# Dividing the last PSUM copy between ScalarE and VectorE, with fewer counting instructions, in a batched matrix product

## The chip, the cores and the metric

One core of one Trainium2 chip. The metric is the device time of a whole execution in microseconds (us), taken as the median of several runs. "Span" is the profiler's time from the first to the last instruction of one execution, 1.8 us less than the device time here.

## The reference

```python
batch, m, k, n = 16, 512, 768, 1024          # x: (16, 768, 512), y: (16, 768, 1024), fp32
def reference(x, y):
    return np.einsum('bkm,bkn->bmn', x, y).astype(np.float32)
```

## The kernel before

Per batch, SyncE loads x (1.5 MB) and y (3 MB), VectorE casts both to bf16, TensorE runs 48 matmuls of 512 columns in two groups, ScalarE copies each group out of PSUM (the memory of the tile ps, which the matmuls write), and SyncE stores the 2 MB result. In the trace all transfers go through one hardware queue (q1 on the page: 4512 packets, 109.05 MB), they land in the order in which SyncE issues them, and each ends in 16 landings (768 for the 48 transfers), which I take as one from each of the 16 DMA engines.

```python
NO = 5                                                        # five output buffers ob
ps = [psum [P, HB=2, NT=2, NF=512] fp32 for i in range(2)]    # a group: 2 blocks of 1024 fp32 a partition
...
    for _ in range(60):                                       # the counting instructions
        nc.vector.sem_inc(idle, 1)
    for b in range(B):                                        # casts
        ...
        nc.vector.tensor_copy(yb[:, i, ks], ys[i][:, ks]).then_inc(cast, 1)
...
    nc.scalar.nop().then_inc(room, 2)
    for _ in range(60):
        nc.scalar.sem_inc(idle, 1)
    for b in range(B):
        if b >= NO:
            nc.scalar.wait_ge(so[b % NO], 16 * (b // NO))     # the buffer's last store has landed
        for g in range(2):
            nc.scalar.wait_ge(groups, 2 * b + g + 1)          # the matmuls of this group are done
            cp = nc.scalar.copy(ob[b % NO][:, g * HB:(g + 1) * HB]..., ps[g][:])
            if b < B - 1:
                cp.then_inc(room, 1)
        ...
    section.close()                                           # all engines meet here
    nc.sync.dma_start(o_v[B - 1], ob[(B - 1) % NO][:])        # the last store
```

Nothing ever waits for `idle`: the counting instructions only shift what comes after them (in the trace they take 0.067 us each on ScalarE and 0.093 on VectorE). In the queue, blocks of four stores stand between the loads, and at the end the stores of batches 8 to 14 stand one behind the other, with the store of batch 15 after the closing barrier.

## Time and profile before

| | before |
|---|---|
| device time, median of 3 runs | 260.51 us (260.50 to 260.77) |
| span of the profiled run | 258.8 us |
| bytes moved | 109.05 MB, DMA engines busy 98.6% of the span |
| matmuls end / last copy ends / last store issued | 249.58 / 251.48 / 251.67 us |
| last data packet ends / span ends | 257.57 / 258.8 us |

The prediction below shows the lines that carry this. A line of the timeline reads: start, duration, engine, line of the program, operation, output from input, and in brackets the idle time ahead of it with what ended it. I also use two kinds of record beneath those views: the DMA packets (start, duration, size) and the landings (the 16 semaphore increments per transfer). For the last store the 16 landings come 0.38 to 0.46 us after the ends of the 16 rows of packets in the kernel before and 0.33 to 0.47 in the changed one, both in order of time, so I read the spread of the landings as how far the DMA engines have drifted apart. The records do not number the engines.

### The profile page before, as it was taken

To read this page: it belongs to the slowest core of one execution; us is meant where nothing else is said; L and a number is where in the kernel's file an instruction comes from. 1 tells how busy PE (TensorE), PEld (TensorE's weight loads), DVE (VectorE), ACT (ScalarE), POOL (GpSimd) and SP (SyncE) were. 2 spreads that over 40 slices of the span, in tenths; PEclk is the share of its full clock that TensorE was granted. 3 is DMA by queue.
4 is the path that set the end of the run, shared out by engine and by line. 5 is a ranking of instruction groups with operands and counts; after the bars stand their busy time and mean duration, and the time that the engine had idled before them with its cause. 6 is when DMAs were issued, how large, how long until landed. Compare 5 with 4: busy or idle time off the path is not lost. (4 is left out here: it accounts for less than half of the span.)

```text
span 258.8 us, 2506 instructions
## 1 busy us (share of the span) xinstructions
PE 181.6 (70%) x768; PEld 89.3 (34%) x768; DVE 82.0 (32%) x33; ACT 60.9 (24%) x33; POOL 0.2 (0%) x4
## 2 busy tenths in 40 slices
PE   0009999999999006999499920899669980099950
PEld 0004555554545002454145500355325530035520
DVE  0261645527164350011734525002255262300000
ACT  1000442234220005222214002324402200413430
POOL 0000000000000000000000000000000000000000
PEclk9999999999999855899779985699979995569995
DMA  7999989899999999999999989999899999999987
GB/s 273 424 475 410 471 380 479 372 479 395 456 410 441 387 418 430 466 446 418 433 433 425 471 352 443 420 461 479 372 479 403 448 410 390 433 438 420 436 357 324
DMA packets 4514, 109.07 MB, mean 421 GB/s; under 512 B 768, under 2 KB 768, under 8 KB 768
## 3 DMA queue, kind: packets, MB, share of 16 engines
q1 hardware_dynamic: 4512, 109.05, 98.6%
q14 instruction: 2, 0.02, 0.0%
HBM read 75.50 MB, written 33.55 MB: 421 GB/s over the span
## 5 line engine op out<-in xcount | busy, mean ns | idle before, releaser
L157 PE MATMUL ps<-yb,xb 128*128 x768 | 181.6, 402 | 68.0 <-PEq L152 68.0
L157 PEld LDWEIGHTS ps<-yb,xb 128*128 x768 | 89.3, 116 | 159.8 <-issue 89.8
L173 ACT COPY ob<-ps 128x2048 f32<-128x2048 f32 x32 | 59.6, 1872 | 185.3 <-PE ps L157 125.2
L135 DVE CAST yb<-ys 128x6144 bf16<-128x6144 f32 (+1 forms) x17 | 53.8, 3172 | 77.8 <-DMA ys<-in_y_dram 77.8
L131 DVE CAST xb<-xs 128x3072 bf16<-128x3072 f32 x16 | 28.2, 1761 | 62.5 <-DMA xs<-in_x_dram 48.7
L173 ACT ACT_TABLE_LOAD x1 | 1.3, 1283 | 5.3 <-issue 5.3
L203 POOL MEMSET const-bfloat16-1.0<- 128x1 bf16 x1 | 0.1, 103 | 0.0
L203 POOL MEMSET const-uint8-127<- 128x1 uint8 x1 | 0.1, 102 | 0.0
L203 POOL MEMSET const-float32-0.0<- 128x1 f32 x1 | 0.1, 100 | 0.2 <-issue 0.2
L203 POOL MEMSET const-float32-1.0<- 128x1 f32 x1 | 0.1, 99 | 0.0
## 6 DMA issues: line engine op xcount, KB each, us to landing
ys<-in_y_dram SPq DMA_DIRECT2D x16, 3072.0 KB, 18.6
out_dram<-ob SPq DMA_DIRECT2D x16, 2048.0 KB, 27.2
xs<-in_x_dram SPq DMA_DIRECT2D x16, 1536.0 KB, 20.1
```

The lines of the kernel that those rows point to most:

```text
L131: nc.vector.tensor_copy(xb[:, i], xs[i][:]).then_inc(cast, 1)
L135: nc.vector.tensor_copy(yb[:, i, ks], ys[i][:, ks]).then_inc(cast, 1)
L157: mm = nc.tensor.matmul(ps[g][:, m, nt], x_w[:, bass.ds(s, 1), kt, mo], yb[:, bass.ds(s, 1), kt, nt * NF:(nt + 1) * NF], start=(kt == 0), ...
L173: cp = nc.scalar.copy(ob[b % NO][:, g * HB:(g + 1) * HB].rearrange("p m (t f) -> p m t f", f=NF), ps[g][:])
L203: nc = _bacc.Bacc("TRN2", target_bir_lowering=False, num_devices=1)
```

## The change

The intent is to shorten the last step ahead of the last store: VectorE, idle by then, takes one block of the last group while ScalarE copies the other. The counting instructions fall from 60 to 16 on each of the two engines.

```diff
-    for _ in range(60):
+    for _ in range(16):
         nc.vector.sem_inc(idle, 1)
...
+    nc.vector.wait_ge(so[(B - 1) % NO], 16 * ((B - 1) // NO))
+    nc.vector.wait_ge(groups, 2 * B)
+    nc.vector.tensor_copy(ob[(B - 1) % NO][:, MT - 1].rearrange("p (t f) -> p t f", f=NF), ps[1][:, HB - 1])
...
-    for _ in range(60):
+    for _ in range(16):
         nc.scalar.sem_inc(idle, 1)
...
-            cp = nc.scalar.copy(ob[b % NO][:, g * HB:(g + 1) * HB].rearrange("p m (t f) -> p m t f", f=NF),
-                                ps[g][:])
+            h = HB if (b, g) < (B - 1, 1) else HB - 1
+            cp = nc.scalar.copy(ob[b % NO][:, g * HB:g * HB + h].rearrange("p m (t f) -> p m t f", f=NF),
+                                ps[g][:, :h])
```

## The prediction

> **What bounds the kernel now.** I read the page first (span, busy slices, queues), then the chain of waits, then the timeline of the last 60 us, and last the trace's single records of semaphores and DMA packets.

> The page of the kernel before:

> ```profile
> span 258.8 us, 2506 instructions
> PE 181.6 (70%) x768; PEld 89.3 (34%) x768; DVE 82.0 (32%) x33; ACT 60.9 (24%) x33; POOL 0.2 (0%) x4
> PEclk9999999999999855899779985699979995569995
> DMA  7999989899999999999999989999899999999987
> q1 hardware_dynamic: 4512, 109.05, 98.6%
> q14 instruction: 2, 0.02, 0.0%
> ```

> The 16 DMA engines are busy for 98.6% of the span and move 109.05 MB: for almost the whole time this kernel is bound by its transfers, and VectorE (32%) and ScalarE (24%) have room. Only the edges of the DMA row, the leading 7 and the closing 8 and 7, leave something to win. The queue of instructions made two transfers; they return below. The PEclk row shows half clock after TensorE's pauses, at the 5 5 6 near the end too.

> The chain that ended last, in order of time:

> ```profile
> 225.71 0.27 issue
> 225.98 23.61 PE ps L157 x96
> 249.59 0.02 issue
> 249.61 1.87 ACT ob L173
> ```

> So the end hangs on the matmuls of the last two batches and then on one ScalarE copy of 1.87 us, the copy that the change cuts. The timeline shows what stands ahead of and behind it:

> ```profile
> 202.04 1.87 ACT L173 COPY ob<-ps 128x2048 f32<-128x2048 f32 x1 [3.25 <-PE ps L157]
> 202.04 1.76 DVE L131 CAST xb<-xs 128x3072 bf16<-128x3072 f32 x1 [1.80 <-PE ps L157]
> 207.87 3.36 DVE L135 CAST yb<-ys 128x6144 bf16<-128x6144 f32 x1 [4.07 <-DMA ys<-in_y_dram]
> ...
> 223.74 3.63 ACT L173 COPY ob<-ps 128x2048 f32<-128x2048 f32 x2 [19.83 <-DMA out_dram<-ob]
> ```

> ```profile
> 244.49 1.87 ACT L173 COPY ob<-ps 128x2048 f32<-128x2048 f32 x1 [3.37 <-PE ps L157]
> 249.61 1.87 ACT L173 COPY ob<-ps 128x2048 f32<-128x2048 f32 x1 [3.26 <-PE ps L157]
> 251.67 0.33 SPq L188 DMA_DIRECT2D out_dram<-ob  x1
> ```

> The copy ends at 251.48, the final 2 MB store is issued at 251.67 (0.19 us of barrier), its first data packet starts at 252.50 (0.83 us after the issue), its last ends at 257.57, and the span ends at 258.8. Two things in the packet records decide how much an earlier issue is worth. Fourteen of the 16 engines finish the store of batch 14 between 251.45 and 251.84, so they idle for 0.7 to 1.1 us. The other two finish it at 252.41 and 252.45 and hardly idle at all. In the final store each engine moves 8 packets of 16 KB, 0.61 us each, 4.9 us in all.

> The row at 223.74 shows the same coupling once more: ScalarE had waited 19.83 us for the store of batch 8 to land, so that a buffer came free, and TensorE's start at 225.98 hangs on that copy.

> [...] The trace before has no VectorE read of PSUM, [...] a cast of 3072 takes 1.76 us and one of 6144 takes 3.36, that is 0.52 ns an element and 0.16 us fixed. [...]

> [...]

> [...] the two refills in the span, at 8.97 and 10.91 us, are packets of 8 KB[...].

> [...] the first group of batch 14 takes 8.06 us from 225.98, full clock comes back at 231.48, and each later group takes 5.34.

> **The change part by part.** (1) The last ScalarE copy shrinks from 2048 to 1024 elements a partition. Half of 1.87 is 0.93; with a fixed part of up to 0.2 us kept, about 1.02 us. It is on the path. (2) VectorE gets a copy of 1024 fp32 out of PSUM[...]. It waits for the same semaphore as ScalarE, and the rows at 202.04 show that both engines start within the same 0.01 us on such a release. VectorE has been idle since 222.3. So the pair ends at 249.61 + 1.23 = 250.84 instead of 251.48: 0.64 us saved, with VectorE now the later of the two. (3) The closing barrier: before, SyncE had collected VectorE's and TensorE's drains at 249.66 and waited for ScalarE alone. Now VectorE's arrives last and SyncE asks for it first, so one semaphore step that used to be hidden, about 0.06 us between neighbouring SyncE records, comes after it. Issue at 250.84 + 0.19 + 0.06 = 251.09, so 0.58 us earlier. (4) From there to the end. First data could come at 251.09 + 0.83 = 251.92. The fourteen engines are then nearly all free, but the two late ones start their eight packets at about 252.45 as their queues allow, and end at 252.45 + 4.92 = 257.37 instead of 257.57. Worth 0.20 us if they stay late, the full 0.58 if they do not.

> (5) The 44 counting instructions fewer on each engine. They cost 0.067 us each on ScalarE and 0.093 on VectorE, 3.0 and 4.1 us together, but off the path: VectorE's ended at 6.46, the first x load's last engine reported at 7.15, and the first cast began at 7.18. ScalarE's first copy is at 26.4. No saving there. What they do move is the refill of instructions. ScalarE's even steps of 0.067 us have one gap, of 0.377, ahead of its 64th instruction, the last count; VectorE's 64th is its first cast. The two refills follow about 4 us later. With 44 fewer, the 64th instruction becomes, by counting, VectorE's cast of the last x (at 212.4) and ScalarE's second last copy (at 244.5). Both have slack: the y behind that cast lands at 218.8, and that ScalarE copy ends over 3 us before the next group is done. So a hiccup of 0.3 us in each is hidden. But a refill also holds up the one DMA engine that carries it: the data packets behind the two refills began 0.3 us late and took 1.16 and 1.46 us against the usual 0.91, so 0.55 and 0.86 us each, and on queues that never empty such a delay stays. At least one of the two late engines may be late for this reason. Moving the refills may free them, or make others late nearer the end.

> Sum: between 0.20 and 0.58 us for the copy, and 0 to 0.3 on top if an earlier landing of batch 8 lets TensorE start earlier. I take 0.38 us of 260.51, which is 260.13.

> **The rivals.** (a) The late DMA engines eat the gain: the store is issued 0.58 us earlier, yet the end moves 0.2. For it: the two end times above[...]. Time 260.3. (b) The refills' move frees those engines: full gain and an earlier start of TensorE. For it: the delays at 8.97 and 10.91. Against it: the stores stay in the queue ahead, so the end cannot come before 251.84 + 4.92 = 256.76, 0.8 us at most. Time 259.7. (c) A refill stalls the last copy or the barrier: for it, the second last ScalarE copy is only one instruction from the boundary by my count. 0.3 to 1 us lost: 260.5 to 261. (d) VectorE's read of PSUM is slower than estimated; beyond 1.87 us it would undo the change. Against it: ScalarE's 0.91 ns an element from the same memory. [...]

> **Range and chances.** The middle is 260.13. The smallest plausible gain, with the spread of the runs (260.5 to 260.77), gives 260.6; the largest, (b), gives 259.7. Two per cent is 5.2 us, six times what the gap at the end can yield; slower by 5 us would need a stall that nothing in the profile suggests. So within 2% at 0.98.

> **What would show it.** Right: a ScalarE copy of about 1.02 us and a VectorE copy of about 1.23 in the timeline, both from about 249.6; the last store's issue about 0.6 us earlier against the end of the matmuls; the end of the data only 0.2 to 0.6 earlier; two 8 KB refills late instead of at 9 and 11 us. Wrong: the chain ends in a wait or in a VectorE copy over 1.5 us; a gap ahead of the last copies; TensorE's start of batch 14 moved by more than 0.7 us.

Passages that no trace or run of this case shows are cut from the prediction where marked. The rate behind VectorE's 1.23 us in step (2) was an assumption of mine: with that 1.23 us the sum came to 0.20 to 0.58 us for the copy, of which it took 0.38, and so to 260.13. That the two copies would not slow each other was an assumption too; side by side they took 1.01 and 1.23 us.

What the two traces show of the rest: ScalarE's copies of 2048 and of 1024 elements took 1.87 and 1.01 us in the changed kernel, so by my estimate the fixed part in step (1) is 0.15 us (twice 1.01 less 1.87). I call "refill" an 8 KB packet in the queue that the page calls "instruction"; each kernel of the two has two in its span, each 3.5 to 3.7 us after the 64th recorded instruction of VectorE or ScalarE. That it brings instructions is my reading of the queue's name. The data packet behind each took 1.16 and 1.46 us in place of 0.91 in the kernel before, and 2.48 in place of 1.83 and 0.73 in place of 0.61 in the changed one. A delay stayed: in the kernel before the spread of the landings was 0.64 us ahead of the refills at 8.97 and 10.91 us and then 1.15 to 1.17 in the fourteen transfers that landed from 14.96 to 84.61 us; in the changed kernel, without refills there, it was 0.81 and then 0.79 to 0.80.

## The result, and the profile after

| | before | changed |
|---|---|---|
| device time, median of 6 runs each | 260.61 us (260.45 to 260.77) | 260.62 us (260.43 to 260.81) |
| ratio, changed over before | | 1.000 (95%: 0.9987 to 1.0013) |
| span of the profiled run | 258.8 us | 258.7 us |
| matmuls end | 249.58 us | 249.50 us |
| last store issued | 251.67 us | 251.11 us |
| ninth of the 16 engines ends its last packet | 257.49 us | 256.95 us |
| last of the 16 engines ends its last packet | 257.57 us | 257.41 us |

A ratio here is the mean time of one kernel's fast runs over the mean of the other's in the same rounds, so it is not quite the ratio of the medians.

The chain that ended last in the changed kernel, in order of time (start, us, what):

```profile
225.50 0.27 issue
225.77 23.75 PE ps L161 x96
249.51 0.03 issue
249.54 0.02 DVEq L138
249.56 0.04 issue
249.61 1.23 DVE ob L139
```

The VectorE copy has taken the place of ScalarE's at the end of the chain. Its waits are an instruction of their own (DVEq L138), so it starts 0.07 us after ScalarE's half, which the timeline of the changed kernel shows:

```profile
244.72 1.87 ACT L179 COPY ob<-ps 128x2048 f32<-128x2048 f32 x1 [3.68 <-PE ps L161]
249.54 1.01 ACT L179 COPY ob<-ps 128x1024 f32<-128x1024 f32 x1 [2.94 <-PE ps L161]
249.61 1.23 DVE L139 COPY ob<-ps 128x1024 f32<-128x1024 f32 x1 [27.51 <-PE ps L161]
251.11 0.33 SPq L194 DMA_DIRECT2D out_dram<-ob  x1
```

1.01 and 1.23 us are the durations that the prediction had, and the store is issued 0.56 us earlier; counted from the end of the matmuls it is 1.61 us in place of 2.09. The copy did what it should. The next two fences give the last microseconds in stretches (first number pair: the stretch; then its length, TensorE's granted clock (1.00 is full speed), busy share of the DMA engines by packets started in it, GB/s). Before:

```profile
250.00:251.00 1.00, 1.00 0.80 344
251.00:252.00 1.00, 0.98 0.35 148
252.00:253.00 1.00, 0.50 0.62 262
253.00:256.00 3.00, 0.50 1.03 437
256.00:257.00 1.00, 0.50 1.23 524
```

Changed:

```profile
250.00:251.00 1.00, 1.00 0.84 360
251.00:252.00 1.00, 1.00 0.77 328
252.00:253.00 1.00, 0.51 0.88 377
253.00:256.00 3.00, 0.50 1.04 437
256.00:257.00 1.00, 0.50 0.66 279
```

The hole at 251 to 253 (148 and 262 GB/s) has largely closed, and in return the last microsecond is half empty (279 in place of 524): the bytes moved earlier, the end did not. In the packet records 14 of the 16 engines end between 256.87 and 257.01 us, one at 257.12, and one at 257.41. That one engine finished its part of the store of batch 14 only at 252.53, 0.6 us after the last store's first packets on the others (251.94), so the earlier issue could not help it. This is where the gain went. In the kernel before, by contrast, all 16 engines end between 257.44 and 257.57: the two late ones were through the store of batch 14 (252.41 and 252.45) just as the last store's first packets came (252.50), so the issue and the late engines set the end together. A later issue then shows in full, an earlier one by no more than the 0.2 us that the late engines leave (252.45 and 4.92 us of packets make 257.37).

### The profile page after: what moved, and what is told of

It is laid out like the page before. It is cut to its first block, busy times and chain, and to the rows that moved or that the text cites. A ratio compares the mean times of both kernels' runs of the same rounds, so it can differ in the third digit from the quotient of the medians.

```text
span 258.7 us, 2420 instructions
## 1 busy us (share of the span) xinstructions
PE 179.3 (69%) x768; PEld 89.0 (34%) x768; DVE 83.2 (32%) x34; ACT 60.0 (23%) x33; POOL 0.2 (0%) x4
## 3 DMA queue, kind: packets, MB, share of 16 engines
q1 hardware_dynamic: 4512, 109.05, 98.7%
## 5 line engine op out<-in xcount | busy, mean ns | idle before, releaser
L161 PE MATMUL ps<-yb,xb 128*128 x768 | 179.3, 398 | 70.2 <-PEq L156 70.2
L179 ACT COPY ob<-ps 128x2048 f32<-128x2048 f32 (+1 forms) x32 | 58.7, 1845 | 188.5 <-PE ps L161 126.8
L135 DVE CAST yb<-ys 128x6144 bf16<-128x6144 f32 (+1 forms) x17 | 53.8, 3172 | 79.4 <-DMA ys<-in_y_dram 79.4
L131 DVE CAST xb<-xs 128x3072 bf16<-128x3072 f32 x16 | 28.2, 1760 | 60.7 <-DMA xs<-in_x_dram 48.8
L139 DVE COPY ob<-ps 128x1024 f32<-128x1024 f32 x1 | 1.2, 1225 | 27.5 <-PE ps L161 27.5
```

The source lines that it names most:

```text
L131: nc.vector.tensor_copy(xb[:, i], xs[i][:]).then_inc(cast, 1)
L139: nc.vector.tensor_copy(ob[(B - 1) % NO][:, MT - 1].rearrange("p (t f) -> p t f", f=NF), ps[1][:, HB - 1])
L161: mm = nc.tensor.matmul(ps[g][:, m, nt], x_w[:, bass.ds(s, 1), kt, mo], yb[:, bass.ds(s, 1), kt, nt * NF:(nt + 1) * NF], start=(kt == 0), ...
L179: cp = nc.scalar.copy(ob[b % NO][:, g * HB:g * HB + h].rearrange("p m (t f) -> p m t f", f=NF), ps[g][:, :h])
```

## The experiments

Theory L (late queue): the end is set by the DMA engine that is last through its queue of stores, so an earlier issue only fills the idle gap of the others. Theory O (offset): the copy gains about 0.5 us and the moved refills of instructions lose as much. A second question is why one engine is late.

The traces of the first eight runs and of the two last ones, all in us. "Spread" is the last landing less the first, for the store of batch 8 and of batch 14:

| run | matmuls end | last store issued | ninth engine ends | last engine ends | spread, store 8 | spread, store 14 |
|---|---|---|---|---|---|---|
| before | 249.58 | 251.67 | 257.49 | 257.57 | 1.44 | 1.65 |
| changed | 249.50 | 251.11 | 256.95 | 257.41 | 1.21 | 1.73 |
| a1_again | 249.87 | 251.48 | 257.32 | 257.77 | 1.32 | 1.85 |
| a2_copy_only | 249.35 | 250.96 | 256.83 | 257.62 | 1.00 | 1.77 |
| a3_counts_only | 248.88 | 250.97 | 256.83 | 257.67 | 1.15 | 2.01 |
| a4_split_no_counts | 249.06 | 250.66 | 256.58 | 257.34 | 0.94 | 1.62 |
| b1_free_store | 249.66 | 241.64 | 256.69 | 257.54 | 1.15 | 1.71 |
| b2_idle_pe | none | 248.25 | 256.45 | 256.89 | 0.83 | 1.01 |
| b4_copy_twice | 249.87 | 253.73 | 259.55 | 259.63 | 1.45 | 1.73 |
| c3_short_whole | 248.79 | 250.88 | 256.70 | 256.78 | 1.19 | 1.58 |
| c4_short_split | 248.92 | 250.53 | 256.35 | 256.43 | 1.17 | 1.54 |

### a1_again: the changed kernel once more

No edit.

> The changed kernel itself once more, for a tighter interval. Theory L (late queue): the end is set by the one DMA engine that is last through its queue of stores, so the 0.56 us by which the last store is issued earlier closes the idle gap of the other engines and moves the end by only 0.1 to 0.2 us: ratio to before 0.9992 to 0.9997. Theory O (offset): copy gains about 0.5 us and the moved refills of instructions lose the same: ratio 1.000 here, and the two parts alone tell.

260.77 us against 260.58 (9 runs of before, 260.38 to 260.98); ratio 0.9999 (0.9986 to 1.0013). The result stands: no difference that these runs can see. The interval is 0.35 us to either side, so it can't tell theory L's 0.1 to 0.2 us from nothing. Averaged over both comparisons, the 11 runs of the changed kernel are at 260.63 us and the 15 of before at 260.61, a difference of 0.02 us give or take 0.12 (1.96 standard errors). Single traces can't tell it either: this one ends its last packet at 257.77, the first trace of the same kernel at 257.41 and that of before at 257.57. What follows has to come from runs that change the end by more.

### a2_copy_only and a3_counts_only: the two parts alone

The first edit keeps 60 counting instructions in the changed kernel; the second puts 16 in the kernel before.

```diff
 a2_copy_only (from the changed kernel)      a3_counts_only (from the kernel before)
-    for _ in range(16):   (both engines)    -    for _ in range(60):   (both engines)
+    for _ in range(60):                     +    for _ in range(16):
```

> Only the divided copy, 60 counting instructions kept, so the refills are at about 9 and 11 us as before. Theory L: issue of the last store 0.55 us earlier against the end of the matmuls, last data packet 0.1 to 0.25 us earlier, ratio 0.9990 to 0.9997. Theory O: the copy's whole gain shows, 0.5 us, ratio about 0.998.

260.67 us, ratio 1.0002 (0.9988 to 1.0015).

> Only the 16 counting instructions, with the undivided copy. Refills at about 215 and 248 us. Theory L: the idle gap of 0.7 to 1 us ahead of the last store swallows what the refills delay, so the end is as before, ratio 0.9995 to 1.0005. Theory O: 0.5 us slower, ratio about 1.002.

260.68 us, ratio 0.9999 (0.9986 to 1.0013). Theory O falls: it wanted 0.998 and 1.002, and 0.998 lies outside the first interval, 1.002 outside the second. My number for a2, a last packet 0.1 to 0.25 us earlier, was not met either (257.62 against 257.57), although the store was issued 0.71 us earlier.

a3 adds something that I had not asked for. Its TensorE finished 0.99 us earlier than that of a1, most of it through the clock:

a1_again:

```profile
226.07 23.81 PE ps L161 x96
```

a3_counts_only:

```profile
225.66 23.23 PE ps L157 x96
248.92 1.86 ACT ob L173
```

TensorE took 0.58 us less for the same 96 matmuls, as full clock came back after 4.7 us in a3 (at 230.39) and after 5.9 us in a1 (at 231.98), and it started 0.41 us earlier. With the undivided copy of 1.86 us a3 still issued its last store half a microsecond before a1, and yet its last packet ended only 0.10 us earlier. In this pair of traces the end does not follow the matmuls, within the limits of this queue.

### a4_split_no_counts: no refills of instructions among the stores

```diff
-    for _ in range(16):   (both engines, in the changed kernel)
+    for _ in range(0):
```

> The divided copy with no counting instructions: neither engine reaches its 64th instruction before the closing barrier, so no refill packet inside the stores. If the refills make the late engines late (a part of theory L): one late engine fewer, last landing of the store of batch 8 0.2 to 0.6 us earlier against the others, end 0.3 to 0.6 us ahead of before, ratio 0.9977 to 0.9988. If lateness has another cause: as the changed kernel, within 0.1 us of it.

260.73 us, ratio 1.0006 (0.9993 to 1.0020). The trace has no refill packet in the span, and at the store of batch 8 the spread is the smallest of the ordinary runs, 0.94 us. But between the stores of batches 8 and 14 one engine's lag still grows, to 1.62 us, and the last packet ends at 257.34 against the 257.41 of the changed kernel. So the refills are not what makes the engine late at the end; the prediction's rival (b) needed that. The 0.3 to 0.6 us did not come.

### b1_free_store: the last store waits for no copy at all

Wrong result: the store sends the buffer of batch 13 and stands right behind the store of batch 14.

```diff
     for b in range(B - FIRST + TURN, B - 1):
         store(b)
+    nc.sync.dma_start(o_v[B - 1], ob[(B - 3) % NO][:]).then_inc(last, 16)
...
+    nc.sync.wait_ge(last, 16)
     section.close()
-    nc.sync.dma_start(o_v[B - 1], ob[(B - 1) % NO][:])
```

> Wrong result on purpose: the last store sends the finished buffer of batch 13 and stands directly behind the store of batch 14 in the queue, so it waits for no matmul, no copy and no barrier; 60 counts, undivided copy. This is the ceiling of what any quicker copy of the last block can give. Theory L (late queue): the ordinary engines end near 256.8 us but the late one near 257.4 as in the changed kernel, time within 0.3 us of before (the closing barrier now comes after the data and adds 0.2 to 0.5 us), ratio 0.999 to 1.002. Rival (the barrier or the copy still sets the end): last packet over 0.6 us earlier than 257.4, and a time below 260.2.

The timeline of this run:

```profile
241.64 1.07 SPq L122 DMA_DIRECT2D out_dram<-ob  x1
244.58 1.87 ACT L175 COPY ob<-ps 128x2048 f32<-128x2048 f32 x1 [3.37 <-PE ps L159]
249.70 1.86 ACT L175 COPY ob<-ps 128x2048 f32<-128x2048 f32 x1 [3.26 <-PE ps L159]
```

The store is issued at 241.64, ten microseconds before that of the kernel before and 8 us ahead of the last copy, and its last packet ends at 257.54, against 257.57. No quicker copy can do better than no copy, so the ceiling of the whole idea lies within 0.2 us or so of nothing in these traces (the changed kernel and a4 ended at 257.41 and 257.34, the changed kernel's second trace at 257.77). The time is 261.11 us, ratio 1.0018 (1.0004 to 1.0031): inside the ratio that I had put, but by the medians 0.59 us above before in place of 0.3 at most. From the last packet to the end of the span it takes 1.79 us in place of 1.24, because the barrier now comes after the data.

### b2_idle_pe: the stores without TensorE beside them

Wrong result, undivided copy, no counts: TensorE leaves out batches 14 and 15.

```diff
-    with nc.Fori(0, B // 2, engines=pe):
+    with nc.Fori(0, B // 2 - 1, engines=pe):
-            nc.scalar.wait_ge(groups, 2 * b + g + 1)
+            nc.scalar.wait_ge(groups, min(2 * b + g + 1, 2 * B - 4))
 (the last stores wait for ScalarE's count of finished batches in place of groups)
```

> Wrong result on purpose: TensorE leaves out batches 14 and 15, ScalarE copies old blocks; no counts, undivided copy. If one DMA engine grows late because TensorE is at work while the stores run (theory P): the last landing of the last six stores stays within 1.0 us of the first one, none grows, and the last packet ends about 0.6 us earlier than in the run without counts (257.34), at 256.7 to 256.9. If that engine is slow in storing by itself (theory I): its lateness grows by 0.15 us a store as before, to 1.6 us, and the last packet ends at 257.3 to 257.5.

260.27 us, ratio 0.9986 (0.9971 to 1.0001). The spread goes from 0.83 to 1.01 us in place of 0.94 to 1.62, and the last packet ends at 256.89, 0.45 us before a4's. Theory I, an engine that is slow by itself, falls. The packet records make it plain: between 227.5 and 243 us, of about 400 store packets of 16 KB, which take 0.611 us as a rule, 15 took 0.625 us or more in the kernel before and 20 in a4, but none in this run. The stores moved the same bytes at the same rate (stretch, length, TensorE, weight loads, VectorE, ScalarE, GpSimd, clock, DMA share, GB/s), in the kernel before:

```profile
226.00:250.00 24.00, 23.58 (x96) 11.25 (x96) 0.00 (x0) 7.37 (x5) 0.00 (x0) 0.89 1.02 434
```

and with TensorE idle:

```profile
226.00:250.00 24.00, 0.00 (x0) 0.00 (x0) 0.00 (x0) 8.21 (x5) 0.00 (x0) 0.50 1.02 435
```

So the transfers as a whole ran alike with TensorE at work and idle (434 and 435 GB/s); one DMA engine did not. That it is one, and the one that matters, the packets of a4 show: all 21 that took 0.62 us or more between 227.5 and 243 us lie in one row of packets in which each starts within 0.01 us of the end of the one before it, and this row ends with the last packet of all, at 257.34. In the changed kernel 19 of 20 lie in such a row, which ends at 257.41.

### b3_half_matmuls: twice the instructions for the same product

From the kernel before without counts. Right result.

```diff
-                for kt in range(KT):
+                for q, kt in [(q, kt) for q in range(2) for kt in range(KT)]:
...
+                        c = slice(q * NF // 2, (q + 1) * NF // 2)
                         mm = nc.tensor.matmul(
-                            ps[g][:, m, nt], x_w[...],
-                            yb[:, bass.ds(s, 1), kt, nt * NF:(nt + 1) * NF],
+                            ps[g][:, m, nt, c], x_w[...],
+                            yb[:, bass.ds(s, 1), kt, nt * NF + c.start:nt * NF + c.stop],
```

> Right result: each matmul of 512 columns becomes two of 256, so TensorE runs twice the instructions for the same arithmetic; no counts, undivided copy. If lateness follows the number of TensorE's instructions (a form of theory P): it grows by 0.3 us a store, to 2 to 2.6 us at the store of batch 14, and the end is 0.6 to 1.2 us later. If it follows TensorE's data or busy time: growth as before, 0.15 us a store. Theory I: as before too.

262.08 us, ratio 1.0055 (1.0040 to 1.0071). In the same stretch 23 packets took 0.625 us or more (15 in the kernel before, 20 in a4, which has no counts either), and the second latest engine's lag grew from 1.20 us at the store of batch 8 to 2.10 at that of batch 12, 0.22 us a store on average and 0.38 at the last step. The latest engine, already 3.0 us behind since the first 100 us for a reason that I did not look for, hardly moved. After that the queue ran dry, because TensorE was done only at 251.54, so the end at 259.54 is set by the matmuls and the copy and says nothing on lateness. In these traces the lag goes with the number of instructions (311 recorded and 0.79 us of excess here, 183 and 0.42 in a4, by the table under c2) rather than with the arithmetic, which had not changed; the later time (1.4 us by the ratio, 0.6 to 1.2 expected) came mostly another way.

### b4_copy_twice: the change turned round

From the kernel before, with 60 counts. Right result.

```diff
+            if (b, g) == (B - 1, 1):
+                nc.scalar.copy(xs[0][:, :4].rearrange("p (m t) f -> p m t f", t=NT), ps[g][:])
             cp = nc.scalar.copy(ob...
```

> Right result, the opposite of the change: ScalarE reads the last block a second time into an unused buffer ahead of the last copy, which delays the last store by 1.87 us; 60 counts. Theory L: before had at most 0.2 us of slack at its late engine, so nearly the whole delay shows: 1.6 to 1.9 us slower, ratio 1.006 to 1.0073. If the copy does not lie on the path at all: ratio 1.000.

In the trace the last packet ends 9.77 us after the matmuls in place of 7.99, so 1.78 of the 1.87 us show: before had next to no slack. The time, though, is 261.58 us with runs of 260.87, 261.06, 262.11 and 262.61, ratio 1.0028 (1.0005 to 1.0051), less than I expected. The traced run was the one of 262.61 (span 260.8). Part of the difference can come from the clock: in the traces with TensorE at work, full clock comes back 4.3 to 6.0 us after TensorE's start (6.0 in this one), which by my estimate is worth up to 0.9 us (half of the 1.7 us between them), and a3 and a1 show TensorE ending up to 1 us apart. That would not cover the 1.7 us between the outer runs; the quick runs left no trace, so the rest stays open.

### c1_pool_counts and c2_pe_counts: instructions without matmuls

Wrong result. Both start from b2, in which hardly any lag grows, and add a loop of 320 counting instructions from about 227 us on, on GpSimd or on TensorE's sequencer.

```diff
+    nc.gpsimd.wait_ge(outs, 2)                    (c2: nc.tensor)
+    with nc.Fori(0, 40, engines=...):
+        for _ in range(8):
+            nc.gpsimd.sem_inc(idle, 1)            (c2: nc.tensor)
```

> Wrong result on purpose: TensorE again leaves out the last two batches, and GpSimd runs a loop of 320 counting instructions from about 227 us on, beside the last stores. If any engine's stream of instructions (or its record) slows a DMA engine: one engine's lateness grows by 0.1 us a store or more from 227 us on, and 20 or more store packets after it take over 625 ns. If it takes TensorE's work: growth about 0.03 us a store as with TensorE idle, and fewer than 5 such packets.

> Wrong result on purpose: the same with the 320 counting instructions on TensorE's sequencer in place of its matmuls. If TensorE's instructions slow the DMA engine: growth of 0.1 us a store or more, 20 or more packets over 625 ns. If it takes matmuls and weight loads: no growth, fewer than 5.

The loops lasted longer than planned and put the closing barrier off, so the times (270.67 and 300.55 us, one run each) mean nothing here; the stores up to batch 14 do. With GpSimd counting the spread grew from 1.15 to 2.21 us between the stores of batches 8 and 14, the last five steps near 0.2 each; with TensorE's sequencer counting, from 1.06 to 1.78. Neither loop moves any data.

| 227.5 to 243 us | instructions recorded, all engines | store packets of 0.625 us or more | time over 0.611 us, in packets of 0.62 us or more |
|---|---|---|---|
| b2_idle_pe | 7 | 0 | 0.01 us |
| c2_pe_counts | 105 | 14 | 0.31 us |
| before | 184 | 15 | 0.39 us |
| a4_split_no_counts | 183 | 20 | 0.42 us |
| c1_pool_counts | 189 | 25 | 0.64 us |
| b3_half_matmuls | 311 | 23 | 0.79 us |

### c3_short_whole and c4_short_split: the same change with a short queue

Wrong result: the store of batch 13 is left out in the kernel before (with 16 counts) and in the changed kernel, so the queue is empty before the last store.

```diff
     for b in range(B - FIRST + TURN, B - 1):
-        store(b)
+        if b != B - 3:
+            store(b)
...
-    for b in range(B - NO, B - 2):
+    for b in range(B - NO, B - 3):
```

> Wrong result on purpose: the store of batch 13 is left out, so the queue runs dry about 4 us before the last store and no DMA engine can be late; undivided copy, 16 counts. The base for the next. Theory L: the time hardly falls, as the chain matmuls, copy, store still takes 7.9 to 8.0 us from the last matmul's end to the last packet.

> Wrong result on purpose: the same short queue with the divided copy. Theory L: now the whole 0.55 us shows, 7.3 to 7.45 us from the last matmul's end to the last packet, and the time is 0.4 to 0.6 us below the run before it (0.15 to 0.25%, near the noise). If something after the copy holds the end: 7.9 us as before.

259.93 and 259.45 us, ratios to before 0.9980 (0.9965 to 0.9994) and 0.9949 (0.9937 to 0.9960): the intervals do not overlap, and the divided copy is 0.48 us quicker by the medians (0.8 by the two ratios, as two of the six undivided runs took 260.59 and 260.76). The last stretches of the undivided copy:

```profile
250.00:251.00 1.00, 1.00 0.00 0
251.00:252.00 1.00, 1.00 0.62 262
...
256.00:257.00 1.00, 0.50 0.62 262
```

and of the divided one:

```profile
250.00:251.00 1.00, 1.00 0.00 0
251.00:252.00 1.00, 1.00 0.85 360
...
256.00:257.00 1.00, 0.50 0.01 0
```

Here the 262 GB/s of the last microsecond are gone, not merely moved. From the end of the matmuls to the last packet it is 8.00 us undivided and 7.51 divided (7.3 to 7.45 expected): 0.48 us, the whole of what the issue gained. The same change pays in full once the queue is empty ahead of the last store and no DMA engine is behind. Theory L holds.

## Why the prediction was wrong

Right:

- The copies, 1.02 and 1.23 us predicted, were 1.01 and 1.23, although they ran side by side out of PSUM from 249.61 to 250.55 us. The change was small, as the chances had it.
- The refills moved to 215.39 and 248.25 us, and the 64th instructions were the two that the count named (the cast at 211.92 and the copy at 244.72). ScalarE's hiccup of 0.31 us is visible ahead of its copy at 244.72, and it was hidden.
- Rival (a), in which the late engines eat the gain, is what happened. Its 0.2 us at the end are not shown: the four traces with the divided copy end at 257.34, 257.41, 257.62 and 257.77 us, against 257.57.

Slightly off: step (2) let both engines start within 0.01 us, but VectorE's two waits took an instruction of their own, 0.07 us; step (3) allowed 0.06 us for the barrier's added step and it was 0.09 (0.28 us from the copy's end to the issue in place of 0.19). The issue gained 0.48 us against the end of the matmuls, not 0.58. One reading was wrong without harm: of the fourteen ordinary engines none ends the store of batch 14 as late as 251.84. They end between 250.98 and 251.69 and idle for 0.8 to 1.5 us; what was read as two of them at 251.80 and 251.84 are packets of the two late engines, with one more to come. The late ones, on which the term rests, were read rightly.

The step that failed is (4) with the sum behind it. It held both outcomes, 0.20 us if the late engines stay late and 0.58 if not, and the sum took 0.38, half way, plus the hope of an earlier landing of batch 8. The engines stay late: the whole term was nothing that the runs or the four traces could see, and b1, with no copy to wait for at all, still ended at 257.54. The reason given for hope in step (5), that the refills make the engine late, was the weak link: without any refill (a4) one engine still falls behind, by some 0.1 to 0.2 us a store (0.94 to 1.62 us of spread over six stores) while instructions run, and it was that engine, not a refilled one, that ended last. With 0.1 us in place of 0.38 the prediction would have read 260.4. The measured 260.62 is 0.02 above the range, in which the noise of the runs had been given too little room: before itself went from 260.38 to 260.98 in nine runs, and beside the changed kernel it measured 260.61 in place of 260.51.

## What to carry to other kernels

An idle gap of the transfer queue is not one number: look at when each DMA engine finishes the transfer ahead, and credit an earlier issue only with the gap of the one that is last (here 0.8 to 1.5 us at fourteen engines, under 0.1 at the two late ones). Before shortening a step in front of a transfer, ask what the end would be if that step took no time at all; one run with the dependency cut (wrong result, right timing) gives the ceiling. And where a term has two outcomes, find the evidence that decides or widen the range; the middle of the two is the one value that neither gives.
